# GLU as seven block products, forms mixed where the outputs are made, and banks kept for the last stage

## The chip, the core and the metric

The kernel runs on one core of one Trainium2 chip. Its engines work side by side and meet through semaphores: TensorE (PE) multiplies, VectorE (DVE) and ScalarE (ACT) work on tiles, GpSimd (POOL) and SyncE (SP) mostly issue transfers, as ScalarE does too. The metric is the device time of one execution in microseconds (us), the median of some runs. The profile is of one execution of its own.

## The reference

One layer over 1024 prompt tokens and 8 sample tokens (1032 columns), all in float32. Two branches, retention with 8 heads and an S5 state space model, are each multiplied by a gate and projected, then merged. Cut to what matters here:

```python
def layer(x, pos, ...):
    h = rmsnorm(x, g_pre)
    proj = h @ w_in
    q, k, v, za, ub, zb, ga, gb = jnp.split(proj, splits, axis=-1)
    ya, s_ret_new = retention(q, k, v, pos, s_ret)
    ya = (ya * jax.nn.silu(za.astype(F32))).astype(x.dtype) @ w_pa
    yb, s_re_new, s_im_new = s5(ub, ...)       # y = gelu(y); y * sigmoid(y @ w_glu + b_glu)
    yb = (yb * jax.nn.silu(zb.astype(F32))).astype(x.dtype) @ w_pb
    merged = jax.nn.sigmoid(ga) * ya + jax.nn.sigmoid(gb) * yb
    out = merged @ w_out
    return x + rmsnorm(out, g_post), ...
```

`w_in` is 2048 x 10240, `w_glu` 1024 x 1024, `w_pa` and `w_pb` 1024 x 2048, `w_out` 2048 x 2048.

## The kernel before

Activations lie transposed, features on the partitions and the 1032 tokens along the row. A float32 matmul is made of three: weights and activations are each split into a high part (ScalarE copies to fp32r, `whi`) and a low part (VectorE subtracts, `wlo`), and high x high, high x low and low x high are added up in a PSUM bank. `linear` (L256 ff. for `split`, L209 to L211 for `three`) does this for plain products, in thirds of 384, 384 and 264 tokens.

Most of the work uses block products instead. `product` (L880 ff., its matmul is L892) takes pairs of output tiles, splits the tokens into two halves of 516 (`HT`), and makes a 2 x 2 block product with seven multiplications instead of eight (a scheme of Strassen's kind). For this the activations are kept as seven *forms* (`FORMS`: u1, t2, v1, t3, t1, t4, v2, sums and differences of the blocks u1, u2, v1, v2), in 16 tiles `a0` to `a15` (`qslot`); the weights are combined on VectorE (`prep`: s1 to s4), two products ahead. A step is one pair of output tiles, seven products of 24 matmuls of 258 columns. The results go through `evac_st` or `evac_p`, which add and subtract PSUM banks into the four output blocks 11, 22, 21, 12.

In order of time:

- the first `ub` tiles by `linear`; then `steps` (L813): 35 pairs of `w_in` columns, twice, once for each half (`kh` 0 and 1) of the 2048 inputs. The partial sums of `kh` 0 go to `pt_d` in DRAM, those of `kh` 1 are added to them by an accumulating transfer (L946), and four products later (`LAG`) the activation, the RoPE or the like is put to work through `at` and `late_work`.
- beside that, in `slot()` after each product, a background generator goes on: `s5_params` and `s5_all` (S5 itself), `order_y` (L1209, brings S5's output into token order and writes `yn_d`), and `retention` (L1159, heads 0 to 7; `head` is L1032). The first head loads its vT and kT itself, each later one was loaded by the head before it (`load_vk`, on POOL's queue).
- GLU (L1475 to L1478): eight output tiles by `linear` from eight split tiles of `yn_d` (`load_gy`, `split_gy`). Beside it `glu_forms` reads `ya_d` back and makes four of the seven forms for `w_pa` in place; the others go to `fa_d`, to be fetched.
- pa and pb: eight steps each. `make_forms` reads `yb_d` and writes `fb_d` in the pa steps; the forms are fetched by `stage` (POOL's queue) into a pool of eight buffers and split by `unstage` into their `a` tiles as the old forms are used up. `gated` multiplies by the gates and, in pb, adds pa's result; for the last pair (p = 7) three of four such additions run on GpSimd.
- the last stage: `out_rows` for tokens 640 and up (`linear`, one bank of 392 columns per output tile), `out_tokens` for token tiles 0 to 2 and 3 to 4 with weights as the moving operand. PSUM is laid out anew before it (L1622): three double banks `pst` and two `pms` before, then five `pmm` and three `pms`.

Buffers come from pools stacked from the left and the right of SBUF. A tile in a new pool waits until what lay there has been released. Weights for block products come through a pool `wst` of seven buffers, four per step, loaded by SP (`fetch`, L842).

Of the kernel before, what the change touches and what calls it, by code (L numbers as in the profile page):

```python
# [23 lines left out]
H = 8  # L24
# [54 lines left out]
def emit(ctx, tc, I, O):  # L79
# [63 lines left out]
    fb_d = dram("fb_d", [2, 4, 128, TOK])  # L143
    yb_d = dram("yb_d", [8, 128, TOK])
# [659 lines left out]
    wstack, wst = popen("wst", "right", 7)  # L804
# [21 lines left out]
    def stage(pool, kh, n, i, eng=P):  # L826
        r = stq[kh, n, i] = pool.tile([128, HT], F32, name="stg")
        if kh in (0, 1):
            src = fm_d[kh, n, i]
        else:  # L830
            y, F = (ya_d, fa_d) if kh == "pa" else (yb_d, fb_d)
# [178 lines left out]
    def ret_const():  # L1010
        for n, shape in (("col", [128, 4, H]), ("mask", [128, 128])):
# [8 lines left out]
        K["a"] = act.tile([128, 2, TOK], F32, name="a12")  # L1020
        K["b"] = act.tile([128, 2, TOK], F32, name="a13")
# [3 lines left out]
    def load_vk(h):  # L1025
        vT, kT = R("vT", [128, TOK]), R("kT", [128, TOK], 2)
        P.dma_start(vT, v_d[h])
        for a in range(2):
            P.dma_start(kT[64 * a:64 * a + 64], kq_d[0, h // 2, a, 64 * (h % 2):64 * (h % 2) + 64])
        return vT, kT  # L1030

    def head(h):  # L1032
# [4 lines left out]
        vT, kT = K.pop("next") if h else load_vk(h)  # L1037
# [89 lines left out]
        if h + 1 < H:  # L1127
            K["next"] = load_vk(h + 1)
# [16 lines left out]
        oo = R("ktS", [128, TOK])  # L1145
# [12 lines left out]

    def retention():  # L1159
        ret_const()  # L1160
        for h in range(H):
            yield from head(h)
# [36 lines left out]
    TAGS = [12, 13, 14, 15] + list(range(12))  # L1199
    xs = {}  # L1200

    def xs_new(k):
        xs[k] = act.tile([128, 2, TOK], F32R, name=f"a{TAGS[k]}")
        return xs[k]

    gys = []
    gyr = {}

    def order_y():  # L1209
        for m in range(8):  # L1210
# [6 lines left out]
            o = k2p["pool"].tile([128, TOK], F32, name="yo", bufs=1)  # L1217
# [7 lines left out]

    def load_gy(m):
        gyr[m] = gp.tile([128, TOK], F32, name="gy")
        nc.sync.dma_start(gyr[m], yn_d[m])

    def split_gy(m):  # L1230
        t = xs_new(m)
        split((t[:, 0, :], t[:, 1, :]), gyr.pop(m))
        gys.append(t)
# [9 lines left out]
    e = 2 * NP - 1  # L1243
    when = {(e - 1, 4): (0,), (e - 1, 5): (1,), (e, 0): (2,), (e, 1): (3, 4), (e, 2): (5,), (e, 3): (6,), (e, 4): (7,)}
    for s in range(2 * NP):
# [35 lines left out]
        if s == 2 * NP - 2:  # L1281
            drain()
            rstack.close()
            gstack, gp = popen("gp", "left", 6)
            for m in range(6):
                load_gy(m)
        for n in range(7):
# [4 lines left out]
            if s == e and n == 5:  # L1292
                todo.extend((I["w_glu"], m, kq) for m in range(8) for kq in range(2))
                fetch_w()
# [15 lines left out]
            if (s, n) in when:  # L1310
                for m in when[s, n]:
                    at(g, lambda m=m: split_gy(m))
                    if m < 2:
                        at(g, lambda m=m: load_gy(6 + m))
            late_work(g)
            slot()
    gstack.close()

    def left_over():
        for n in range(12):  # L1320
            yield
            for g in sorted(due):
                if n >= {1: 4, 2: 6, 3: 9}[g - 14 * NP]:
                    late_work(g)


    bglu = const.tile([128, 8], F32, name="bglu")
    A.dma_start(bglu, I["b_glu"])
    gpost = const.tile([128, KD], F32, name="gpost")
    A.dma_start(gpost, I["g_post"])  # L1330
    zstack, zzp = popen("zz", "left", 4)
    zz_tile = lambda: zzp.tile([128, HT], F32, name="zz")
    opened = {}

    def fx_open():
        opened["fx"], opened["fxp"] = popen("fx", "left", 4)

    def stg_open(bufs):
        opened["stg"], opened["stgp"] = popen("stg3", "left", bufs)

    def glu_forms():
        t = {}

        def ld(i):
            t[i] = [opened["fxp"].tile([128, TOK], F32, name="fx") for _ in range(2)]
            for x, k in zip(t[i], (i, 4 + i)):
                P.dma_start(x, ya_d[k])

        ld(0)
        ld(1)  # L1350
        for _ in range(10):
            yield
        for i in range(4):
            u, v = t.pop(i)
            u1, u2, v1, v2 = u[:, 0:HT], u[:, HT:TOK], v[:, 0:HT], v[:, HT:TOK]
            split(qslot("pa", 0, i), u1)
            sub(u1, u1, u2)
            yield
            split(qslot("pa", 2, i), v1)
            sub(u2, u2, v2)  # L1360
            yield
            add(v2, v2, u1)
            P.dma_start(fa_d[0, i, :, 0:HT], u1)
            split(qslot("pa", 1, i), v2)
            yield
            sub(v1, v1, v2)
            P.dma_start(fa_d[1, i, :, 0:HT], v1)
            split(qslot("pa", 3, i), u2)
            yield
            if i < 2:  # L1370
                yield
                yield
                ld(i + 2)
            yield
        opened["fx"].close()
        stg_open(8)
        for o in order_q[16:24]:
            stage(opened["stgp"], "pa", *o)

    def make_forms(src, F):  # L1380
# [12 lines left out]
        for i in range(4):  # L1393
            u, v = t.pop(i)
            u1, u2, v1, v2 = u[:, 0:HT], u[:, HT:TOK], v[:, 0:HT], v[:, HT:TOK]
            sub(u1, u1, u2)
            sub(u2, u2, v2)
            yield
            add(v2, v2, u1)
            sub(v1, v1, v2)  # L1400
            P.dma_start(F[0, i], u)
            P.dma_start(F[1, i], v)
# [7 lines left out]

    zyq = deque()

    def load_zy(k):
        if k < 24:
            t0, t1 = THIRDS[k % 3]
            z = zz_tile()[:, 0:t1 - t0]
            zyq.append(z)
            P.dma_start(z, zy_d[k // 3, :, t0:t1])

    def evac_glu(m):  # L1420
        def f(t, ps):
            t0, t1 = THIRDS[t]
            s = ETILE(("p1", "u2", "u3")[t])[:, 0:t1 - t0]
            A.activation(s, ps, AF.Sigmoid, bias=bglu[:, m:m + 1])
            mul(s, s, zyq.popleft())
            P.dma_start(yb_d[m, :, t0:t1], s)
            load_zy(3 * m + t + 4)
        return f

    def both():  # L1430
        a, b = left_over(), glu_forms()
        n = 0
        while True:
            live = False
            for x in (a, b):
                try:
                    next(x)
                    live = True
                except StopIteration:
                    pass  # L1440
# [443 lines left out]
```

## Time and profile before

| | |
|---|---|
| median of three runs | 2610.0 us |
| the runs | 2617.08, 2610.0, 2609.98 us |
| the profiled execution | 2613.67 us |
| its span | 2611.9 us |
| VectorE, ScalarE, GpSimd busy | 71%, 37%, 26% of the span |
| DMA moved | 500.25 MB, mean 192 GB/s |

A span runs from the first to the last recorded instruction; the execution's time has a little around it. In rows of groups a line number is that of the helper that emits the operation (L84 is every `tensor_tensor`), so the names of the tiles tell what it is: `wlo<-wraw,whi` is the low part of a weight, `u<-acc,p` an evacuation. Matmuls overlap in the records, each lasting longer than the distance to the next; a rate is counts over the length of a stretch. The stages of the second half lie, in us from the start of the span, about so: `kh` 1 from 1020, retention 1350 to 1772, GLU 1819 to 1909, pa and pb to 2232, `out_rows` to 2373, `out_tokens` to 2600.

### The profile page before, as it was taken

How to read it: one execution, taken by the hardware profiler on the slowest of the kernel's cores; microseconds unless marked ns; L12 is line 12 of the kernel's file. 1: busy time of each engine (PE TensorE's matmuls, PEld its weight loads, DVE VectorE, ACT ScalarE, POOL GpSimd, SP SyncE). 2: the span in 40 equal slices, each digit the busy share in tenths (PEclk: the TensorE clock that was granted, in tenths of full speed). 3: DMA queues.
4: the chain of work that ended last, by engine and by line, in shares of the span. 5: the costliest groups of instructions: out<-in, count | busy, mean ns of one | idle time of the engine just before them, and what ended most of it. 6: DMA issues, size and time to landing. Idle time of an engine off the chain costs nothing.

```text
span 2611.9 us, 51326 instructions
## 1 busy us (share of the span) xinstructions
PE 2588.0 (99%) x19652; PEld 2531.1 (97%) x19652; DVE 1856.4 (71%) x3872; ACT 956.0 (37%) x1679; POOL 688.8 (26%) x1137
## 2 busy tenths in 40 slices
PE   9999999999999999999999999999999999999998
PEld 8999999999999999999999999999999999998886
DVE  7655988898898877558877666666577878544555
ACT  6113232333323324443234444445332422443344
POOL 0103322222222222332234434333422221111011
PEclk9999999999999999999999999999999999999999
DMA  6896534444444447886778878778867786655666
GB/s 192 257 265 217 154 111 125 138 120 124 129 122 131 131 127 245 207 206 168 164 192 241 231 197 209 206 196 250 273 226 255 232 230 212 215 166 182 187 200 227
DMA packets 229909, 500.25 MB, mean 192 GB/s; under 512 B 32432, under 2 KB 54912, under 8 KB 229536
## 3 DMA queue, kind: packets, MB, share of 16 engines
q0 software_dynamic: 90352, 263.82, 36.2%
q1 hardware_dynamic: 103072, 179.57, 22.5%
q10 hardware_dynamic: 36240, 53.60, 7.0%
q8 instruction: 154, 2.52, 0.4%
q14 instruction: 91, 0.75, 0.1%
HBM read 340.57 MB, written 156.30 MB: 190 GB/s over the span
## 4 chain that ended last, share of the span: by engine, by line
PE 97%; DVE 1%; issue 1%; DMA 1%; ACT 0%; DVEq 0%; SPq 0%; POOLq 0%; POOL 0%; ACTq 0%
PE acc L892 65%; PE mm L1782 7%; PE mm L209 5%; PE mm L210 5%; PE mm L211 5%; PE misc L1782 2%; PE acc L209 1%; PE acc L210 1%; PE acc L211 1%; PE misc L634 1%; PE misc L712 1%; PE misc L711 1%; PE misc L1099 1%; PE misc L1089 1%; PE misc L1068 1%
## 5 line engine op out<-in xcount | busy, mean ns | idle before, releaser
L892 PE MATMUL acc<-a,whi 128*128 128x258 f32 x9632 | 1561.4, 284 | 1.0 <-ACT whi L873 0.6
L892 PEld LDWEIGHTS acc<-a,whi 128*128 128x128 f32 x9632 | 1325.8, 190 | 5.2 <-issue 2.6
L892 PE MATMUL acc<-a,wlo 128*128 128x258 f32 x4816 | 969.1, 282 | 0.0
L892 PEld LDWEIGHTS acc<-a,wlo 128*128 128x128 f32 x4816 | 744.7, 189 | 0.0
L84 DVE TENSOR_TENSOR wlo<-wraw,whi 128x512 fp32r<-128x512 f32 x482 | 332.0, 689 | 237.9 <-ACT whi L202 138.1
L873 ACT CAST whi<-wraw 128x512 fp32r<-128x512 f32 x344 | 213.5, 621 | 619.6 <-PE acc L892 481.1
L873 ACT CAST whi<-wr 128x512 fp32r<-128x512 f32 x258 | 160.0, 620 | 507.4 <-PE acc L892 445.3
L209 PE MATMUL mm<-a,whi 128*128 128x384 f32 (+2 forms) x704 | 234.2, 334 | 8.6 <-ACT whi L202 5.2
L210 PE MATMUL mm<-a,whi 128*128 128x384 f32 (+2 forms) x704 | 233.7, 332 | 0.0
L211 PE MATMUL mm<-a,wlo 128*128 128x384 f32 (+2 forms) x704 | 232.2, 330 | 0.0
L84 DVE TENSOR_TENSOR wlo<-wr,whi 128x512 fp32r<-128x512 f32 x273 | 187.2, 686 | 51.6 <-ACT whi L873 30.0
L1782 PE MATMUL mm<-whi,a 128*128 128x512 f32 x512 | 171.1, 395 | 0.0
L202 ACT CAST whi<-wraw 128x512 fp32r<-128x512 f32 x138 | 85.5, 620 | 208.2 <-PE mm L210 104.1
L209 PEld LDWEIGHTS mm<-a,whi 128*128 128x128 f32 x704 | 133.6, 190 | 9.2 <-ACT whi L202 5.2
L211 PEld LDWEIGHTS mm<-a,wlo 128*128 128x128 f32 x704 | 133.9, 190 | 0.4 <-DVE wlo L84 0.2
L210 PEld LDWEIGHTS mm<-a,whi 128*128 128x128 f32 x704 | 133.3, 189 | 0.4 <-DVE a L363 0.4
L84 DVE TENSOR_TENSOR wraw<-wr 128x512 f32<-128x512 f32 x172 | 118.1, 686 | 2.9 <-DMA wr<-in_w_pa 0.6
L1782 PEld LDWEIGHTS mm<-whi,a 128*128 128x128 f32 x512 | 96.1, 188 | 22.8
L84 DVE TENSOR_TENSOR p<-acc,p 128x516 f32<-128x516 f32 x86 | 59.6, 692 | 70.9 <-PE acc L892 70.7
L84 DVE TENSOR_TENSOR wlo<-wx,whi 128x512 fp32r<-128x512 f32 x76 | 52.5, 692 | 71.4 <-ACT whi L202 71.1
L84 DVE TENSOR_TENSOR u<-acc,u 128x516 f32<-128x516 f32 x86 | 59.7, 694 | 60.0 <-PE acc L892 58.7
L84 DVE TENSOR_TENSOR u<-acc,p 128x516 f32<-128x516 f32 x86 | 59.5, 692 | 59.0 <-PE acc L892 58.7
(374 smaller groups left out, 3449.3 us busy)
## 6 DMA issues: line engine op xcount, KB each, us to landing
wr<-in_w_in SPq DMA_DIRECT2D x280, 256.0 KB
pt_d<-u POOLq DMA_DIRECT2D x70, 258.0 KB, 3.2
u<-pt_d POOLq DMA_DIRECT2D x70, 258.0 KB, 5.3
wraw<-in_w_outB SPq DMA_DIRECT2D x66, 256.0 KB
stg<-fm_d POOLq DMA_DIRECT2D x44, 258.0 KB, 4.5
wx<-in_w_outB SPq DMA_DIRECT2D x43, 256.0 KB
wraw<-in_w_out SPq DMA_DIRECT2D x39, 256.0 KB
pt_d<-st POOLq DMA_DIRECT2D x35, 258.0 KB, 3.3
```

Of the source, the lines that this page charges most:

```text
L84: return (eng or V).tensor_tensor(out, a, b, op)
L202: anchor["a"] = A.copy(hi, raw).ins
L209: T.matmul(ps, wh[:, i, :], xh[:, t0:t1], start=first, stop=False)
L210: T.matmul(ps, wh[:, i, :], xl[:, t0:t1], start=False, stop=False)
L211: anchor["p"] = T.matmul(ps, wl[:, i, :], xh[:, t0:t1], start=False, stop=last).ins
L634: T.matmul(ps[0:16, g * 128:(g + 1) * 128], B1[:, g, :], W3[:, g, 0:8, :], start=True, stop=True)
L711: T.matmul(o, Tm[:, g, :], U[:, g, 0:136], start=True, stop=False)
L712: T.matmul(o, W3[:, g, 1:9, :], X[:, g, 0:136], start=False, stop=True)
L873: anchor["a"] = A.copy(hi, f).ins
L892: anchor["p"] = T.matmul(ps[:, j, 0:258], a[:, i, :], b[:, 258 * j:258 * j + 258], start=first and i == 0 and a is wh and b is xh, stop=n ...
L1068: T.matmul(ps[:, c * 128:(c + 1) * 128], kt[:, 4 * i + c, :], vt[:, 4 * i + c, :], start=True, stop=True)
L1782: anchor["p"] = T.matmul(ps[c], a, b, start=k == 0 and a is xh and b is wh, stop=k == KD - 1 and a is xl).ins
```

## The change

GLU becomes four steps of block products between `kh` 1 and pa, with forms from `yn_d` and `fg_d`. The forms are mixed where the outputs are still in SBUF: `order_y` and `retention` take tiles or heads in the order 0, 4, 1, 5, 2, 6, 3, 7, and after each second one `mix` makes the sums of the pair and writes them to `fg_d` or `fa_d`. `transition` replaces the special code for fetching forms: into GLU, into pa and into pb alike, two loads and two splits per product. `wst` has five buffers instead of seven. The last stage stays on the banks `pst` and `pms`; each group of `out_tokens` takes one double bank and, for three token tiles, half of another.

```diff
-    wstack, wst = popen("wst", "right", 7)
+    wstack, wst = popen("wst", "right", 5)
...
-    steps = [(kh, p) for kh in range(2) for p in range(NP)] + [(kh, p) for kh in ("pa", "pb") for p in range(8)]
-    lim = [14 * NP]
+    steps = [(kh, p) for kh in range(2) for p in range(NP)] + [(kh, p) for kh, n in (("glu", 4), ("pa", 8), ("pb", 8)) for p in range(n)]
+    lim = [7 * len(steps)]
...
-        j = (2 * n + i // 2 + {0: 0, 1: -2, "pa": 4, "pb": 2}[kh]) % 16
+        j = (2 * n + i // 2 + {0: 0, 1: -2, "glu": -4, "pa": -6, "pb": -8}[kh]) % 16
...
     def ret_const():
+        K["a"] = act.tile([128, 2, TOK], F32, name="a12")
+        K["b"] = act.tile([128, 2, TOK], F32, name="a13")
+        K["next"] = load_vk(0, A)
         for n, shape in (("col", [128, 4, H]), ("mask", [128, 128])):
...
-        vT, kT = K.pop("next") if h else load_vk(h)
+        vT, kT = K.pop("next")
...
-        if h + 1 < H:
-            K["next"] = load_vk(h + 1)
+        if h != HEADS[-1]:
+            K["next"] = load_vk(HEADS[HEADS.index(h) + 1])
...
-        oo = R("ktS", [128, TOK])
+        oo = K["oo", h] = rstd if h < 4 else R("oo", [128, TOK])
...
+    HEADS = [0, 4, 1, 5, 2, 6, 3, 7]
+
     def retention():
         ret_const()
-        for h in range(H):
-            yield from head(h)
+        f = iter(())
+        for h in HEADS:
+            for _ in head(h):
+                yield
+                next(f, None)
+            if h > 3:
+                f = mix(K["oo", h - 4], K["oo", h], fa_d, h - 4)
+        for _ in f:
+            yield
...
+    def mix_a(u, v):
+        sub(u[:, 0:HT], u[:, 0:HT], u[:, HT:TOK])
+        sub(u[:, HT:TOK], u[:, HT:TOK], v[:, HT:TOK])
+
+    def mix_b(u, v, F, i):
+        add(v[:, HT:TOK], v[:, HT:TOK], u[:, 0:HT])
+        sub(v[:, 0:HT], v[:, 0:HT], v[:, HT:TOK])
+        P.dma_start(F[0, i], u)
+        P.dma_start(F[1, i], v)
+
+    def mix(u, v, F, i):
+        for _ in range(3):
+            yield
+        mix_a(u, v)
+        yield
+        mix_b(u, v, F, i)
+        yield
...
-        for m in range(8):
+        for m in (0, 4, 1, 5, 2, 6, 3, 7):
...
+            if m > 3:
+                yield from mix(yo[m - 4], yo[m], fg_d, m - 4)
...
+    def transition(g, base, kind):
+
+        q = g - 7 * base
+        n = moved.setdefault(kind, [0, 0])
+
+        def load():
+            at(g, lambda o=order_q[n[0]]: stage(opened["stgp"], kind, *o))
+            n[0] += 1
+
+        if 0 <= q < 4:
+            load()
+            load()
+        if 3 <= q < 20:
+            for i in range(1 if q < 7 else 2):
+                if n[1] < 28:
+                    at(g, lambda o=order_q[n[1]]: unstage(kind, *o))
+                    n[1] += 1
+                    if n[0] < 28:
+                        load()
...
-    raw_of["pool"] = wst
-    for m in range(8):
-        linear(I["w_glu"], m, 8, pair(gys), evac_glu(m), tick=glu_tick(m))
-    drain()
-    raw_of.clear()
...
-        if kind == "pb" and p > 1:
+        if kind == "pb" and p > 1 and (p < 7 or c):
...
+        if kind == "glu":
+            def times():
+                mul(t, t, z)
+                P.dma_start(yb_d[m, :, cols], t)
+
+            A.activation(t if ps is None else two(t), t if ps is None else ps, AF.Sigmoid, bias=bglu[:, m:m + 1])
+            at(g + 1, times)
+            return
...
-            add(t, t, zq.pop((name, "p")), P if p == 7 and name != "12" else V)
+            add(t, t, zq.pop((name, "p")), V)
...
-        a = act.tile([128, 2, TOK], F32R, name=f"a{m}")
+        a = act.tile([128, 2, TOK], F32R, name=f"a{(6 + m) % 16}")
...
+            transition(g, 2 * NP - 2, "glu")
+            transition(g, SG + 2, "pa")
+            transition(g, SB - 2, "pb")
...
-    psum_layout(("pmm", 5), ("pms", 3))
...
-            ps = [mmbank() if c < 2 else misc() for c in range(nch)]
+            both_ = banks_of["pst"].tile([128, 2, 512], F32, name="acc")
+            ps = [both_[:, 0, :], both_[:, 1, :]]
+            if nch == 3:
+                ps.append(mmbank())
             steps = [[(k, c) for c in range(nch)] for k in range(KD)]
             if last and g == 3:
+                ps[1] = mmbank()
                 steps[13:] = [[(k, c) for k in (13, 14, 15)] for c in range(nch)]
+            elif not last:
+                steps[14:] = [[(k, c) for k in (14, 15)] for c in range(nch)]
```

Here `SG` is the first GLU step (70), `SA` = `SG` + 4 the first of pa and `SB` = `SG` + 12 the first of pb. Gone with GLU's `linear` are `load_gy`, `split_gy`, `glu_forms`, `load_zy`, `evac_glu` and their helpers.

More of the change, by code (lines that the diff above doesn't have):

```diff
@@ L143, in emit @@
     fb_d = dram("fb_d", [2, 4, 128, TOK])
+    fg_d = dram("fg_d", [2, 4, 128, TOK])
     yb_d = dram("yb_d", [8, 128, TOK])
@@ L1198, in emit @@
     k2p = {}
[L1199 to L1207, printed above, removed]
+    def mix_a(u, v):
[13 more added lines that the diff above has]
+        yield
     def order_y():
-        for m in range(8):
+        yo = {}
+        for m in (0, 4, 1, 5, 2, 6, 3, 7):
             r = k2p["pool"].tile([128, TOK], F32, name="yr", bufs=1)
@@ L1216, in order_y @@
                 yield
-            o = k2p["pool"].tile([128, TOK], F32, name="yo", bufs=1)
+            o = yo[m] = k2p["pool"].tile([128, TOK], F32, name="yo", bufs=2)
             for c in range(2):
@@ L1242, in emit, with fx_open, stg_open @@
     nxt = done_q = 0
-    e = 2 * NP - 1
-    when = {(e - 1, 4): (0,), (e - 1, 5): (1,), (e, 0): (2,), (e, 1): (3, 4), (e, 2): (5,), (e, 3): (6,), (e, 4): (7,)}
+    bglu = const.tile([128, 8], F32, name="bglu")
+    A.dma_start(bglu, I["b_glu"])
+    gpost = const.tile([128, KD], F32, name="gpost")
+    A.dma_start(gpost, I["g_post"])
+    opened, moved = {}, {}
+    def fx_open():
+        opened["fx"], opened["fxp"] = popen("fx", "left", 4)
+    def stg_open(bufs):
+        opened["stg"], opened["stgp"] = popen("stg3", "left", bufs)
+    def transition(g, base, kind):
[14 more added lines that the diff above has]
+                        load()
     for s in range(2 * NP):
@@ L1283, in emit @@
             rstack.close()
-            gstack, gp = popen("gp", "left", 6)
-            for m in range(6):
-                load_gy(m)
+            zstack, zzp = popen("zz", "left", 4)
+            stg_open(8)
         for n in range(7):
@@ L1409, in make_forms @@
         opened["fx"].close()
[L1411 to L1440, printed above, removed]
-            if not live:
-                return
-            yield
-    def tail_forms():
-        for k in (1, 1, 2):
-            for _ in range(k):
-                unstage("pa", *order_q[pa_q[0]])
-                if pa_q[0] + 8 < 28:
-                    stage(opened["stgp"], "pa", *order_q[pa_q[0] + 8])
-                pa_q[0] += 1
-            yield
-    pa_q = [16]
-    pair = lambda L: (lambda k: (L[k][:, 0, :], L[k][:, 1, :]))
-    for k in range(4):
-        load_zy(k)
-    fx_open()
-    bg.append(both())
-    S0 = 2 * NP
-    lim[0] = 7 * len(steps)
-    def glu_tick(m):
-        def f(kq, t):
-            if m == 7 and kq == 0 and t == 2:
-                drain()
-                bg.append(tail_forms())
-                fetch(S0)
-            if m == 7 and kq == 1 and t < 2:
-                prep(7 * S0 + t)
-            if t < 2 or kq == 1:
-                slot()
-        return f
-    raw_of["pool"] = wst
-    for m in range(8):
-        linear(I["w_glu"], m, 8, pair(gys), evac_glu(m), tick=glu_tick(m))
-    drain()
-    raw_of.clear()
     zq = {}
```

122 lines of the change are left out of this document (15 added, 107 removed).

## The prediction

> **What bounds the kernel now.** I read the page first: busy time by engine, then the shares of the chain of work that ended last, then the list of whatever the TensorE waited for in the whole program.
>
> ```profile
> span 2611.9 us, 51326 instructions
> PE 2588.0 (99%) x19652; PEld 2531.1 (97%) x19652; DVE 1856.4 (71%) x3872; ACT 956.0 (37%) x1679; POOL 688.8 (26%) x1137
> PE 97%; DVE 1%; issue 1%; DMA 1%; ACT 0%; DVEq 0%; SPq 0%; POOLq 0%; POOL 0%; ACTq 0%
> ```
> ```profile
> PE mm L209 <- ACT whi L202: 5.2, 1, 5.2
> PE mm L209 <- DVE u L84: 2.8, 1, 2.8
> PE misc L1049 <- ACT a L1047: 2.2, 1, 2.2
> PE acc L892 <- ACT whi L873: 0.6, 1, 0.6
> PE mm L209 <- ACT a L362: 0.5, 1, 0.5
> PE acc L892 <- DVE u L84: 0.3, 2, 0.2
> ```
>
> The reader is to see that TensorE (PE) is busy for 2588 of 2611.9 us, and that its waits add up to 11.6 us, of which the first and the fifth row, 5.7 us, are the start-up (the first weights and the first x). So there are only two ways to gain: fewer matmul columns, or one of the two waits of 2.8 and 2.2 us. And there is one way to lose: a new wait of PE. What the other engines do is free as long as PE doesn't notice.
>
> The windows view of the stretches that matter (start:end; length, then busy time and count for PE, PE weight load, VectorE, ScalarE, GpSimd; granted clock, DMA share, GB/s):
>
> ```profile
> 1818.77:1909.38 90.61, 90.61 (x580) 90.61 (x579) 47.17 (x79) 34.70 (x63) 39.88 (x74) 1.00 0.76 252
> 1909.38:2232.04 322.66, 322.66 (x2689) 322.45 (x2687) 254.96 (x400) 103.36 (x179) 68.59 (x118) 1.00 0.76 239
> 2234.87:2238.64 3.77, 3.77 (x12) 3.77 (x13) 2.74 (x5) 0.00 (x0) 0.54 (x1) 0.55 0.66 221
> 1240.00:1260.00 20.00, 20.00 (x169) 20.00 (x168) 17.28 (x29) 5.32 (x9) 5.73 (x8) 1.00 0.68 156
> 1760.00:1780.00 20.00, 20.00 (x167) 19.81 (x166) 13.39 (x34) 10.41 (x22) 8.38 (x11) 1.00 0.61 157
> 1800.00:1818.00 18.00, 18.00 (x152) 18.00 (x152) 14.03 (x18) 12.54 (x18) 7.20 (x13) 1.00 0.81 214
> 2000.00:2020.00 20.00, 20.00 (x169) 20.00 (x168) 12.88 (x21) 4.84 (x8) 1.99 (x5) 1.00 0.50 157
> 2060.00:2080.00 20.00, 20.00 (x169) 20.00 (x168) 19.96 (x34) 12.02 (x23) 7.91 (x15) 1.00 0.96 318
> ```
>
> **GLU as block products.** The first row is today's GLU: 90.61 us with no gap. Its matmuls by shape, for one of its three lines, then those of the stage after it:
>
> ```profile
> L209 PE MATMUL acc<-a,whi 128*128 128x384 f32 x128 | 43.1, 336 | 0.0
> L209 PE MATMUL acc<-a,whi 128*128 128x264 f32 x64 | 18.3, 286 | 0.0
> L892 PE MATMUL acc<-a,whi 128*128 128x258 f32 x1792 | 288.2, 283 | 0.0
> L892 PE MATMUL acc<-a,wlo 128*128 128x258 f32 x896 | 179.9, 282 | 0.0
> ```
>
> That is 3 x 192 = 576 matmuls, 198,144 columns. The change makes 4 pairs of output tiles x 7 products x 4 blocks x 3 parts x 2 halves = 672 matmuls of 258 columns, 173,376 columns, seven eighths. The pa and pb stage is made of just these: 1792 + 896 = 2688 in 322.66 us, or 0.1200 us each (the mean durations in the rows overlap and are no rate). 672 x 0.1200 = 80.7 us; the saving is **9.9 us**. It is on PE, so on the path; nothing hides it.
>
> What VectorE and ScalarE do for it must stay beside PE. One step of 7 products (7 x 24 x 0.1200 = 20.2 us) asks VectorE for 7 splits, 4 weight sums, 7 evacuations and 4 gate products, 22 operations. Such operations follow each other at 0.61 us (the starts of the two rows at 1437.46 and 1438.06 below), so 13.4 us. In the transition that fetches the forms there are 2 splits per product more, 14 x 0.61 = 8.5, together 21.9 us in 20.2. That is over the mark, but the last window row is this very load, the pb transition: VectorE 19.96 of 20.00 busy, PE 20.00. ScalarE had 12.02; GLU's four sigmoids of a step fit into the other 8. So I cost the two new transitions (into GLU, into pa) at nothing on both. If the cover of two products' lookahead is gone, the excess, 1.7 us each, is what it costs.
>
> Their transfers are another matter. At two loads of 258 KB per product the pb transition raises the DMA share from 0.50 to 0.96, by 0.46. The transition into GLU falls into the last gb steps, whose own share lies between 0.61 and 0.81 (the rows at 1760, which has retention in it, and at 1800, which has other loads in it): 1.07 to 1.27 for the 8 products at two loads, 23 us, which leaves 1.6 to 6.2 us of transfers late. The late one that hurts is the accumulating read of the partial sum:
>
> ```profile
> u<-pt_d POOLq DMA_DIRECT2D x5, 258.0 KB, 7.7
> ```
>
> That median of 7.7 us is from 1776 to 1912; ScalarE asks for it four products, 11.5 us, after issue, and has a product's time (2.9 us) before PE notices. Bounds 0 to 6.2 us; I take 1, nearer to the pb row, which had no wait.
>
> **Banks kept.** The 2.8 us wait is the handover from pst to pmm/pms:
>
> ```profile
> 2231.64 0.40 PE L892 MATMUL acc<-a,wlo 128*128 128x258 f32 x2
> 2234.87 0.48 PE L209 MATMUL mm<-a,whi 128*128 128x392 f32 x1 [2.83 <-DVE u L84]
> 2238.64 0.34 PE L209 MATMUL mm<-a,whi 128*128 128x392 f32 x1
> 2239.17 0.34 PE L209 MATMUL mm<-a,whi 128*128 128x392 f32 x1
> ```
> ```profile
> 2232.36 1.76 DVE L84 TENSOR_TENSOR wlo<-wraw,whi 128x512 fp32r<-128x512 f32 x1
> 2234.04 0.68 DVE L84 TENSOR_TENSOR u<-acc,u 128x516 f32<-128x516 f32 x1
> 2232.05 1.52 POOL L84 TENSOR_TENSOR p<-p,pp 128x516 f32<-128x516 f32 x1 [1.35 <-DVE p L84]
> ```
>
> The first matmul of w_out needs a bank that the last evacuation (u<-acc) frees, and that stood in VectorE's queue behind a split which took 1.76 us instead of 0.68 (the row at 1438.06 below) while GpSimd was adding. Behind the gap the granted clock is 0.55: 12 matmuls took 3.77 us, at the later pace ((2239.17 - 2238.64)/3 = 0.177) they take 2.12. The handover costs 2.83 + 1.65 = 4.5 us. With the banks kept, w_out's first bank is one that was freed four products earlier, and GpSimd's three adds are gone (two become accumulating DMAs, one goes to VectorE). What is late next is the low part of the first w_out weights, the split itself: begun at 2232.36 and not stretched it is done at 2233.0, and PE wants it two matmuls after 2232.04 (2231.64 + 0.40), at 2232.4. The queue ahead of it is shorter, too; I leave 0.4 us: **-4.1 us**; bounds 0 (the wait only changes its name) and -4.5.
>
> The Trainium skill, page "TensorE: Matmul & The Clock Gate", section "Why this matters for your kernels", asks only that there be no idle gaps over about 3 us, since a window of idle lowers the clock. By that rule a gap of 2.83 us would not have cost the clock, and this part would bring 2.4. The trace differs: the clock is halved right behind this gap; the measurement decides.
>
> In the last stage three double banks take turns. At the end of each weight group the last two blocks are taken token tile by token tile, 6 matmuls each, so the second half of a double bank is done 6 matmuls, 1.4 us, before the group ends and wanted 1.4 us after the next begins. Its evacuation is one ScalarE and one VectorE operation of 0.6 to 0.7 us. That fits: 0.
>
> **Retention.** The 2.2 us wait stands at the first head:
>
> ```profile
> 1347.88 0.58 POOL L1013 DMA_DIRECT2D col<-in_col  x1 [1.33 <-DMA kq_d<-pl]
> 1349.51 0.53 POOL L1027 DMA_DIRECT2D vT<-v_d  x1
> 1352.65 0.87 POOL L946 DMA_DIRECT2D st<-pt_d  x1 [1.00 <-ACT st L988]
> 1362.65 1.28 ACT L966 ACT_TABLE_LOAD   x1 [2.16 <-DMA st<-pt_d]
> ```
>
> ScalarE waited for the partial sum, which took 10 us from its issue at 1352.65 behind constants, vT and kT on POOL's queue; the copy that frees PE's misc bank stood behind it. The change issues vT and kT (three transfers, 1 MB) ahead of the constants and from ScalarE's queue. That unloads POOL's queue, but all wait for kq_d<-pl as col did (1347.88), and a ScalarE that stands there holds up the next split and evacuation. Bounds -2.2 and +1.5; I take **-1.0**.
>
> The Trainium skill, page "DMA: Bandwidth & Descriptors", section "Issuing engines are not separate DMA queues", says that transfers from any issuing engine share the same 16 DMA engines, so only issue time is saved. By it this term is 0 and the sum 1.0 us smaller; no row here shows the two cases side by side.
>
> The mixing is 16 subtractions and additions of 516 for S5 and 16 for retention, in pairs of 1.2 us. For S5 they fall into stretches where VectorE has at least 2.7 us idle in 20 (the row at 1240): 0. For retention three of four fall ahead of the scores, VectorE's tightest place in a head:
>
> ```profile
> 1437.46 0.68 DVE L84 TENSOR_TENSOR u<-u,acc 128x516 f32<-128x516 f32 x1
> 1438.06 0.68 DVE L84 TENSOR_TENSOR wlo<-wr,whi 128x512 fp32r<-128x512 f32 x1
> 1443.28 0.70 DVE L84 TENSOR_TENSOR p<-acc,p 128x516 f32<-128x516 f32 x1 [3.40 <-PE acc L892]
> ```
>
> There 2.4 us more stand against an idle 3.40 us that comes only afterwards: 0 to 1.5 each; I take 0.3 x 3, **+1**. The fourth is issued in one piece when the retention ends; PE has matmuls enough: 0. The order of heads adds no work.
>
> **The sum.** -9.9 - 4.1 - 1.0 + 1 + 1 = **-13.0 us**. Against the profiled execution (2613.67 us, span 2611.9, so 1.8 us around it) that is 2600.7, span 2598.9. The profiled execution lies 3.7 us above the median of 2610.0, whose other runs were 2609.98 and 2617.08; against the median it is **2597.0 us**.
>
> **Rivals.** (1) *The bank wait changes its name.* The w_out weights' low part, or ScalarE standing at the load of the merged tiles until the last mg_d store has landed, halts PE instead. For it: the gap was made by VectorE's queue, and that keeps its order. Against: three adds are gone from GpSimd. Without the 4.1: 2601. (2) *The transfers into GLU are late.* Shares over 1 for 23 us; PE waits the full 6.2 us and the clock halves once behind a gap (1.7): 2597 - 1 + 7.9 = 2604. (3) *Slower: five weight buffers instead of seven.* Then the fourth weight tile of a step is fetched only when the split for its sixth product has read the buffer, one product into the second half, and is wanted 4 products later: 11.5 us, less 1.3 for the split, leaves 10.2 until VectorE and ScalarE stand. It is the one edit that acts in all of 88 steps. It decides from 10.2 us landing time on: each 0.3 us that PE waits per step is 26 us, 2597 + 26 = 2623. Against it are the page's medians for transfers of that size, and in the most crowded stretch st<-pt_d took 10:
>
> ```profile
> pt_d<-u POOLq DMA_DIRECT2D x70, 258.0 KB, 3.2
> u<-pt_d POOLq DMA_DIRECT2D x70, 258.0 KB, 5.3
> ```
>
> (4) *GLU brings nothing*, were the stage bound elsewhere: its PE row has no idle, so I give it no chance of its own.
>
> **How the numbers follow.** Forecast 0.62; rival 1 0.18; rival 2 0.14; rival 3 0.04; 0.02 for something unseen. The forecast's own ends: -9.9 - 4.5 - 2.2 = 2593.4 below; above, half of the unknown costs, 2601. The range reaches to rivals 1 and 2: 2592 to 2605. A measurement can tell about 0.3%, 7.8 us, from no change: faster means under 2602.2, which is the forecast, most of rival 1: 0.81; same is rival 2 and the rest of 1: 0.14; slower 0.05.
>
> **What would show it.** GLU about 80.7 us of L892 between the last gb product and the first pa product; no gap and a clock of 1.00 at the start of w_out; a list of PE's waits without the 2.8. Wrong would be: PE waiting for whi or wlo with a wr transfer behind it in many steps (rival 3), for an accumulating read in the two steps ahead of GLU (rival 2), or a gap before the first w_out matmuls (rival 1).

## The result and the profile after

The changed kernel takes 2624.1 us (median of 5 runs, 2621.2 to 2625.6) against 2610.3 of the kernel before on the same chip: a ratio of 1.0045, 95% interval 1.0034 to 1.0057. It is slower, by 12 us by the ratio and 14 by the medians; the forecast was 13 us faster, and the time lies outside its range, 2592 to 2605. The profiled execution took 2625.6 us, 1.5 above the median; that of the kernel before lies 3.4 above its own, so that a difference of two traces can be a few us off that of the medians. The page of after:

```profile
span 2623.8 us, 51705 instructions
PE 2587.1 (99%) x19748; PEld 2523.9 (96%) x19748; DVE 1895.2 (72%) x3949; ACT 968.9 (37%) x1707; POOL 693.3 (26%) x1145
...
L84 DVE TENSOR_TENSOR wraw<-wr 128x512 f32<-128x512 f32 x180 | 123.3, 685 | 28.6 <-DMA wr<-in_w_in 22.9
```

TensorE is busy for only 0.9 us less than before, although 25 thousand columns are gone; 11.0 us of its busy time are now at half clock, 3.4 before. The last row is new: VectorE stands 22.9 us for weights that haven't landed, at the sums of two weight tiles. TensorE's own list of waits (us in total, times, longest):

```profile
PE acc L893 <- DVE u L84: 10.6, 8, 2.7
PE acc L893 <- DVE wlo L84: 5.5, 2, 4.9
PE acc L893 <- ACT p L983: 1.8, 1, 1.8
PE acc L212 <- DVE wlo L84: 0.7, 1, 0.7
```

The 2.8 and 2.2 us of before are gone; 18.6 us of others have come. Where they lie is read by counting matmuls: a step of block products has 168, so the time at which each step starts can be compared in the two traces.

| stretch | before, us | after, us | difference |
|---|---|---|---|
| start to step 45 | 1221.6 | 1221.8 | +0.1 |
| steps 45 to 50 (rotation of q and k) | 121.0 | 132.9 | **+11.9** |
| step 51 (retention's first head) | 24.4 | 31.4 | **+7.0** |
| steps 52 to 67 | 411.5 | 412.0 | +0.5 |
| step 68 (end of retention) | 20.2 | 24.3 | **+4.1** |
| step 69 and GLU | 110.6 | 100.8 | **-9.8** |
| pa and pb | 322.8 | 324.0 | +1.1 |
| handover and `out_rows` | 142.2 | 138.6 | **-3.6** |
| `out_tokens` | 225.6 | 227.4 | +1.8 |
| after the last matmul | 12.0 | 10.7 | -1.4 |

GLU and the two parts of the last stage as windows of after, and the last stage of before (columns as in the prediction):

```profile
1842.50:1923.12 80.62, 80.62 (x674) 80.62 (x673) 66.99 (x106) 45.69 (x78) 26.05 (x49) 1.00 0.81 267
2247.14:2385.78 138.64, 137.90 (x770) 137.58 (x769) 60.62 (x88) 63.46 (x112) 16.95 (x18) 1.00 0.57 177
2385.78:2613.18 227.40, 227.34 (x977) 181.10 (x976) 125.53 (x217) 90.59 (x166) 30.66 (x54) 1.00 0.66 206
```
```profile
2232.04:2374.28 142.24, 139.41 (x769) 139.44 (x769) 61.79 (x88) 63.77 (x112) 18.28 (x18) 0.99 0.53 170
2374.28:2599.87 225.59, 225.58 (x977) 182.01 (x976) 125.44 (x217) 91.37 (x166) 30.62 (x54) 1.00 0.67 207
```

So the two gains came, 13.4 us, and three new losses, 23.1 us, ate them. Each is a place where an engine stands with its queue behind it. In the rotation stretch of after:

```profile
1226.04 0.69 DVE L84 TENSOR_TENSOR wraw<-wr,wraw 128x512 f32<-128x512 f32 x1
1231.14 0.69 DVE L84 TENSOR_TENSOR wraw<-wr 128x512 f32<-128x512 f32 x1 [4.40 <-DMA wr<-in_w_in]
1231.75 0.68 DVE L84 TENSOR_TENSOR u<-p,acc 128x516 f32<-128x516 f32 x1
1232.48 0.75 PE L893 MATMUL acc<-a,whi 128*128 128x258 f32 x4 [1.90 <-DVE u L84]
```

The sum at 1231.14 is `s1` of the *next* step, five products ahead of the first that needs it (through `s2`). It waits for a weight tile, and the evacuation `u<-p,acc` behind it frees TensorE's bank late. At retention's first head:

```profile
1361.42 0.33 ACTq L1029 DMA_DIRECT2D vT<-v_d  x1
1361.85 0.59 ACT L983 COPY p<-acc 128x516 f32<-128x516 f32 x1 [6.55 <-DVE mhalf L1019]
1362.90 0.55 POOL L1021 DMA_DIRECT2D selr<-in_sel  x1
1370.15 0.20 DVE L1023 CAST sel<-selr 128x64 fp32r<-128x64 f32 x1 [6.99 <-DMA selr<-in_sel]
1370.26 0.68 DVE L84 TENSOR_TENSOR wlo<-wraw,whi 128x512 fp32r<-128x512 f32 x1
```
```profile
1348.98 0.54 POOL L1017 DMA_DIRECT2D selr<-in_sel  x1
1352.67 0.20 DVE L1019 CAST sel<-selr 128x64 fp32r<-128x64 f32 x1 [1.06 <-DMA selr<-in_sel]
```

The second fence is the kernel before. After the change the last constant is issued behind the 1 MB of v and k and is there 7.25 us after its issue, not 3.7; VectorE stands at its cast with a weight split behind it. At the end of retention, in after:

```profile
1802.58 0.70 DVE L84 TENSOR_TENSOR oo<-oo,rstd 128x516 f32<-128x516 f32 x1 [4.55 <-DMA ya_d<-oo]
...
1804.78 0.84 POOL L1218 DMA_DIRECT2D fa_d<-oo  x1
1810.67 2.14 POOL L836 DMA_DIRECT2D stg<-yn_d  x4 [4.51 <-issue]
...
1814.41 0.62 ACT L257 CAST a<-stg 128x516 fp32r<-128x516 f32 x1 [5.15 <-issue]
...
1815.06 0.70 DVE L84 TENSOR_TENSOR a<-stg,a 128x516 fp32r<-128x516 f32 x1 [5.39 <-ACT a L257]
...
1815.67 0.69 DVE L84 TENSOR_TENSOR u<-acc,p 128x516 f32<-128x516 f32 x1
```

(`issue` means that the profile shows nothing that was waited for.) The last mix overwrites `oo` while it is still being stored, and the stage loads behind it come late: VectorE stands 5.4 us at the first split into the GLU products, with an evacuation behind it, and TensorE 2.7 us. The store `fa_d<-oo` landed at 1810.06, 0.6 us before the first stage load was issued; in two kernels with an earlier last mix (2623.7 and 2602.8 below) it is 0.6 us again.

### The profile page after: what moved, and what is told of

It is laid out like the page before. It is cut to its first block, busy times and chain, and to the rows that moved or that the text cites. A ratio compares the mean times of both kernels' runs of the same rounds, so it can differ in the third digit from the quotient of the medians.

```text
span 2623.8 us, 51705 instructions
## 1 busy us (share of the span) xinstructions
PE 2587.1 (99%) x19748; PEld 2523.9 (96%) x19748; DVE 1895.2 (72%) x3949; ACT 968.9 (37%) x1707; POOL 693.3 (26%) x1145
## 5 line engine op out<-in xcount | busy, mean ns | idle before, releaser
L893 PE MATMUL acc<-a,whi 128*128 128x258 f32 x10080 | 1638.7, 284 | 13.3 <-DVE u L84 10.6
L893 PEld LDWEIGHTS acc<-a,whi 128*128 128x128 f32 x10080 | 1390.9, 190 | 19.9 <-DVE u L84 8.8
L893 PE MATMUL acc<-a,wlo 128*128 128x258 f32 x5040 | 1016.3, 283 | 5.5 <-DVE wlo L84 5.5
L84 DVE TENSOR_TENSOR wlo<-wraw,whi 128x512 fp32r<-128x512 f32 x496 | 339.8, 686 | 228.0 <-ACT whi L203 132.9
L1680 PE MATMUL acc<-whi,a 128*128 128x512 f32 x640 | 201.9, 396 | 0.0
L210 PE MATMUL mm<-a,whi 128*128 128x384 f32 (+1 forms) x448 | 145.0, 326 | 5.6 <-ACT whi L203 5.6
L1680 PEld LDWEIGHTS acc<-whi,a 128*128 128x128 f32 x640 | 120.2, 188 | 30.1 <-DVE z L84 1.9
L211 PE MATMUL mm<-a,whi 128*128 128x384 f32 (+1 forms) x448 | 145.2, 324 | 0.2 <-DVE a L364 0.2
L212 PE MATMUL mm<-a,wlo 128*128 128x384 f32 (+1 forms) x448 | 144.9, 323 | 0.3 <-DVE wlo L84 0.2
L84 DVE TENSOR_TENSOR wraw<-wr 128x512 f32<-128x512 f32 x180 | 123.3, 685 | 28.6 <-DMA wr<-in_w_in 22.9
L1680 PE MATMUL acc<-wlo,a 128*128 128x512 f32 x320 | 127.0, 397 | 0.0
L84 DVE TENSOR_TENSOR a<-stg,a 128x516 fp32r<-128x516 f32 x140 | 91.7, 688 | 12.8 <-ACT a L257 12.7
L203 ACT CAST whi<-wx 128x512 fp32r<-128x512 f32 x78 | 48.4, 620 | 128.4 <-PE acc L1680 45.0
```

Of the source, the lines that this page charges most:

```text
L84: return (eng or V).tensor_tensor(out, a, b, op)
L203: anchor["a"] = A.copy(hi, raw).ins
L210: T.matmul(ps, wh[:, i, :], xh[:, t0:t1], start=first, stop=False)
L211: T.matmul(ps, wh[:, i, :], xl[:, t0:t1], start=False, stop=False)
L212: anchor["p"] = T.matmul(ps, wl[:, i, :], xh[:, t0:t1], start=False, stop=last).ins
L893: anchor["p"] = T.matmul(ps[:, j, 0:258], a[:, i, :], b[:, 258 * j:258 * j + 258], start=first and i == 0 and a is wh and b is xh, stop=n ...
```

## The experiments

### The rotation stretch

**Five buffers in the kernel before**, and nothing else:

```diff
-    wstack, wst = popen("wst", "right", 7)
+    wstack, wst = popen("wst", "right", 5)
```

> The kernel before with five weight buffers in place of seven, nothing else. Theory (buffers): the sums s1 and s2 of the next step stand five products ahead of where they are needed in VectorE's order, so their tiles 21 and 22 must have landed a whole step early; with five buffers they are asked for one tile's life later and VectorE stands at them, with the evacuation behind it. Then this kernel loses about as much as the changed one did in the six steps from 1212 to 1355: 10 to 12 us, so 2620 to 2622, with TensorE gaps of about 2 us that end with an evacuation u<-p,acc, and VectorE waiting for wr. Rival (mixing): the six waits come from the additional S5 mixing on VectorE in that stretch; then this kernel, which has no mixing there, stays within 3 us of 2610 and shows no gap there.

2617.4 us, ratio 1.0029 (1.0016 to 1.0042): +6.7, steps 45 to 50 +7.5. VectorE's waits there are those of after; the kernel before has none:

```profile
DVE wraw L84 <- DMA wr<-in_w_in: 19.1, 7, 4.4
```

The buffers are a cause by themselves, at two thirds of the expected size in this run.

**Two more buffers in that stretch**, on the changed kernel:

```diff
+            wpool = wsx["p"] if wsx and s <= NP + 15 and wn[0] % 7 > 4 else wst
-            raws[s, n] = wst.tile([128, 4, 128], F32, name="wr")
+            raws[s, n] = wpool.tile([128, 4, 128], F32, name="wr")
...
+            wsx["st"], wsx["p"] = popen("wsx", "left", 2)
...
```

> The changed kernel with two further weight buffers only while the sine and cosine rotation of q and k runs (steps 36 to 50), in memory that is free there; the S5 mixing stays. Theory (buffers): the gaps of TensorE between 1212 and 1355 go, the stretch from step 45 to 51 is 10 to 12 us shorter, and the time is 2612 to 2614. Rival (mixing): the gaps stay, within 3 us of 2624. What follows, the start of retention and the end of it, keeps its own gaps by both.

2610.8 us, ratio 1.0000 (0.9991 to 1.0010): 13 us gained, and steps 45 to 50 are as long as before (0.0), as they are in the four later kernels that have these buffers. The whole 11.9 us hang on the buffers.

**The S5 mixes.** Two kernels ask why the loss is larger in the changed kernel than in the one before with five buffers. One leaves out the S5 mixes' sums, one their stores too:

```diff
-                yield from mix(yo[m - 4], yo[m], fg_d, m - 4)
+                for _ in range(4):
+                    yield
+                P.dma_start(fg_d[0, m - 4], yo[m - 4])
+                P.dma_start(fg_d[1, m - 4], yo[m])
+                yield
```

> The changed kernel with five weight buffers, in which the S5 outputs are stored unmixed: the 16 additions and subtractions of the S5 mixes on VectorE are left out, their stores stay. The kernel before with five buffers lost 7.1 us between steps 45 and 51, the changed kernel 12.0. Theory (VectorE): the other 5 us are the mixes standing ahead of the evacuations on a VectorE that is already late; without them the stretch loses 7, and the time is 2618 to 2620. Rival (transfers): the stores of the mixed forms, 4 MB that the kernel before does not have there, make the weights land later; then the stretch still loses 11 to 12 us.

> The changed kernel with five weight buffers and neither the 16 sums of the S5 mixes nor their 4 MB of stores; the GLU products read the unmixed S5 outputs in place of the mixed ones. It tells whether the larger loss in the changed kernel (13 us by the two more buffers) than in the kernel before with five buffers (7 us) comes from these transfers. Theory (transfers): 2617 to 2619, as the stretch loses about 7. Rival (not the mixes at all): within 2 us of 2624; the sums alone left out gave 2622.7.

2622.7 (1.0042; 1.0027 to 1.0058) and 2620.7 (1.0034; 1.0022 to 1.0047), steps 45 to 50 +8.5 and +4.7. But six kernels whose code is the same up to step 50, the changed one among them, lost 6.4 to 14.3 us there. The intervals overlap that of the changed kernel: how much the mixes add is not settled.

**The weight sums held** behind the last split, with five buffers:

```diff
+            with tc.issue_after(anchor["v"]):
-            add(r[s, name], r[s, a], r[s, b])
+                add(r[s, name], r[s, a], r[s, b])
```

> The changed kernel, still with five weight buffers, with the weight sums s1, s2, s3 and s4 held on VectorE behind the last split that was issued ahead of them; s1 of the next step then stands ahead of the evacuation of product 5 and no longer of product 1. Theory (early sums): it is not that weights land too late for their products, but that VectorE's order asks for them four to five products early; held, the gaps between 1212 and 1355 go, that stretch is 9 to 12 us shorter, and the time is 2612 to 2615, as with two more buffers. Rival (late weights): five buffers are too few in themselves there; the gaps stay or move to another evacuation, and the time is within 3 us of 2624.

2625.7 (1.0058; 1.0046 to 1.0071): no gain, as the rival had it. But its trace has no wait for a weight between 1200 and 1350, and steps 45 to 50 lost 4.3. What was gained there went elsewhere: 4.8 us were lost by step 45, where two evacuations came 1.4 and 1.3 us late in the S5 stretch, and a gap of 3.0 us with the halved clock behind it came at the handover. The first head kept its loss, 7.6 us. So the sums were held only in the rotation stretch, in a kernel that also has the two mends tried below:

```diff
+            with ExitStack() as held:
+                if NP + 2 <= s <= NP + 15:
+                    held.enter_context(tc.issue_after(anchor["v"]))
...
```

> Five weight buffers, the weight sums held only in the rotation stretch (steps 37 to 50), the first head's v and k loaded after the constants from GpSimd's queue, the last mix begun at once. Theory (early sums): the sums' place in VectorE's order is the whole cause of the loss there, so this equals the kernel with two more buffers and the same two mends, 2601 to 2605, with steps 45 to 51 within 2 us of the kernel before. Rival (two causes): with five buffers ScalarE's splits come late too (a 2.3 us gap behind whi was left when all sums were held), the stretch keeps 4 us or more, 2606 to 2610.

2606.4 (0.9979; 0.9970 to 0.9988); steps 45 to 50 +4.4. VectorE's waits in 1200 to 1350, complete:

```profile
DVE wlo L84 <- ACT whi L877: 16.1, 26, 1.1
DVE u L84 <- PE acc L896: 2.3, 3, 1.7
```

In this stretch no weight is late for its product with five buffers; it is late for a sum that stands too early. The 4.4 are in the main one gap of 2.3 us and the halved clock behind it: the held sum `s2` came behind four sums of an S5 mix, and the split waited for it. Both theories had a part.

### The first head of retention

**The early load alone**, in the kernel before:

```diff
     def ret_const():
+        K["a"] = act.tile([128, 2, TOK], F32, name="a12")
+        K["b"] = act.tile([128, 2, TOK], F32, name="a13")
+        K["next"] = load_vk(0, A)
...
```

> The kernel before with only the first head's v and k moved ahead of the constants and to ScalarE's queue, as the change does it. Theory (order): TensorE's gap of 2.2 us at the first head becomes one or two of together 5 to 7 us, part of it behind a split that waits for the cast of the last constant, and the clock is halved behind it: 5 to 8 us slower, 2615 to 2618. Rival (crowding by the rest of the change): within 2 us of 2610, the 2.2 us wait gone or the same. The prediction had put this part at -1.0, from -2.2 to +1.5.

2618.6 (1.0031; 1.0020 to 1.0042): +8 (+5 between the profiled executions), step 51 +5.1. The same picture as in after:

```profile
1347.80 0.59 ACT L982 COPY p<-acc 128x516 f32<-128x516 f32 x1 [4.76 <-DVE mhalf L1018]
1356.15 0.20 DVE L1022 CAST sel<-selr 128x64 fp32r<-128x64 f32 x1 [6.96 <-DMA selr<-in_sel]
1356.99 0.58 PE L892 MATMUL acc<-a,wlo 128*128 128x258 f32 x1 [4.93 <-DVE wlo L84]
```

**Three ways to undo it** in the changed kernel: loading behind the constants from GpSimd's queue; behind them, but from ScalarE's; ahead of them, but from GpSimd's (`load_vk(0, P)`).

```diff
-        K["next"] = load_vk(0, A)
...
         V.tensor_copy(K["sel"], selr.rearrange("p (b c) -> p b c", b=8))
...
+        K["next"] = load_vk(0, P)
```

> The changed kernel with the first head's v and k loaded as before: after the constants, from GpSimd's queue. Theory (order): the early 1 MB of v and k, put ahead of the constants, makes the last constant land late, and VectorE stands at its cast with a weight split behind it; undone, the step from 1355 to 1386 is 6 to 8 us shorter, one wait of about 2 us at the first head is left, and the time is 2616 to 2618. Rival (crowding): the constants are late because the weights and partial sums of this kernel crowd the transfers there, whatever the order; then less than 2 us is gained.

> The changed kernel with the constants issued first, and the first head's v and k still from ScalarE's queue: it tells the order from the queue. Theory (order): what costs is the 1 MB ahead of the last constant, so this gives as much as loading them from GpSimd behind the constants did, 2616 to 2619, and no wait behind the cast of the last constant. Rival (queue): ScalarE standing at an issue that waits for the rotated k costs the time, so it stays within 2 us of 2624.

> The changed kernel with the first head's v and k still ahead of the constants, but from GpSimd's queue. Theory (order): 1 MB ahead of the last constant is enough; VectorE's cast is late by 4 us or more, TensorE stops behind the split, and the time stays at 2622 to 2625; ScalarE's copy no longer waits, which is worth at most 2 us. Rival (queue): ScalarE's queue is what costs, and with GpSimd's queue the step from 1355 to 1386 is 6 us shorter, 2616 to 2618.

2618.3 (1.0024; 1.0013 to 1.0036), 2621.7 (1.0044; 1.0028 to 1.0059) and 2617.0 (1.0022; 1.0013 to 1.0031); step 51: -2.1, +7.8, -0.4. My theory of the order fell twice. Behind the constants in the program is not behind them on the chip when the queue is another one: ScalarE issued v at 1354.4, GpSimd the first constant at 1354.8. And ahead of them it costs nothing in step 51 from GpSimd's queue, although the last constant is just as late:

```profile
1355.77 0.58 ACT L983 COPY p<-acc 128x516 f32<-128x516 f32 x1
1362.11 0.56 POOL L1021 DMA_DIRECT2D selr<-in_sel  x1
1365.14 0.69 DVE L84 TENSOR_TENSOR u<-acc,p 128x516 f32<-128x516 f32 x1 [1.31 <-PE acc L893]
1369.74 0.19 DVE L1023 CAST sel<-selr 128x64 fp32r<-128x64 f32 x1 [3.90 <-DMA selr<-in_sel]
```

It landed after 7.6 us, but in this kernel's order of VectorE the cast stands behind the evacuation of product 3, not of product 1, and ScalarE's copy doesn't wait. That the load makes the constant late holds throughout: in the ten kernels that issue v ahead of it, it landed 6.7 to 8.4 us after its issue, in the nine others 2.9 to 4.6.

**The cast moved** five products later, the load as the change has it:

```diff
             for _ in range(5):
                 yield
+            V.tensor_copy(sel, K["selr"].rearrange("p (b c) -> p b c", b=8))
...
```

> The changed kernel with v and k still loaded ahead of the constants from ScalarE's queue, and only the cast of the last constant on VectorE moved five products later, to where the first head begins. Theory (the cast blocks): TensorE's 4.9 us behind the split that stands behind that cast go, and the halved clock behind them; the step from 1355 to 1386 is 4 to 6 us shorter and the time is 2618 to 2620. The 1.8 us wait for ScalarE's copy, which stands at the loads, stays. Rival (the engines are late anyhow, since weights or partial sums crowd): the gap moves to the next operation and the time stays within 2 us of 2624.

2617.6 (1.0024; 1.0015 to 1.0033): 6.5 us gained, step 51 0.0; of TensorE's waits there, 1.3 us behind ScalarE's copy and 0.6 at the first transpose are left. A late constant is not what cost, but the place of its cast ahead of a split.

### The end of retention

```diff
-        for _ in range(3):
+        for _ in range(0 if F is fa_d and i == 3 else 3):
             yield
         mix_a(u, v)
```

> The changed kernel with the last mix of the retention begun at once, not three products later, so that it is no longer issued in one piece when the retention is closed. Theory (piece): the second half of that mix overwrites oo while oo is still being stored, VectorE stands 4.6 us there with an evacuation behind it, and the memory comes free late; issued sooner, the 4.2 us that step 68 lost go to under 1.5, and the time is 2620 to 2621. Rival (crowding): the transfers into the GLU products are what is late there; then less than 1 us is gained.

2623.7 (1.0046; 1.0030 to 1.0061): step 68 went from +4.1 to +1.6, but GLU gave most of it back. The rival's number holds; its cause, crowded transfers, is not shown. A later start of the splits into GLU, on the mended kernel below:

```diff
-        if 3 <= q < 20:
+        if (5 if kind == "glu" else 3) <= q < 20:
```

> The kernel with the three mends (2602.8) and the first two splits into the GLU products two products later. Theory (loads behind the store): the stage loads wait until the last mix has been stored, land four products on, and the split that waits for them holds up an evacuation; later splits cost nothing and leave no gap around step 68 and 69. In that kernel the gap was already closed, so at most 0.5 us is gained: 2602 to 2603. Rival: the late splits crowd VectorE ahead of the first GLU product and a gap of 1 to 3 us appears at step 70: 2604 to 2606.

2605.2 (0.9977; 0.9967 to 0.9987): 2.4 us above that kernel, which the two intervals don't separate, with gaps of 0.7, 0.7 and 1.4 us from 1807 on; nothing gained, nearer to the rival. What a mended end is worth alone stays open. Step 68 lost 0.0 to 3.8 us in the seven kernels with the mix begun at once, 1.4 to 5.3 in the nine other versions of the changed kernel, but step 69 and GLU gained less in most of the seven (5.4 to 9.8, against 9.8 in each of the nine).

### The banks, and versions that gain

**Three mends together**: two more buffers in the rotation stretch, loading behind the constants from GpSimd, the last mix at once.

> The changed kernel with the two further weight buffers in the rotation stretch, the constants ahead of the first head's v and k on GpSimd's queue, and the last mix begun at once. If the three losses are separate, it takes about 13, 6 and 3 us off 2624: 2601 to 2604, faster than both kernels, which leaves the gain of the block products and of the kept banks. If they share one cause (transfers that crowd everywhere), mending one moves the wait to the next and it stays at 2608 to 2612.

2602.8 us, ratio 0.9968 (0.9956 to 0.9979): faster than both kernels. The losses add up much as separate ones do: alone the three mends gave 13.3, 5.8 and 0.4 us, together 21.3. **The same with the sums held** everywhere in place of the buffers, and **the three mends with the old banks**:

```diff
+    psum_layout(("pmm", 5), ("pms", 3))
...
+            ps = [mmbank() if c < 2 else misc() for c in range(nch)]
```

> The changed kernel with the sums held, the constants ahead of the first head's v and k on GpSimd's queue, and the last mix begun at once; five weight buffers. If holding the sums is worth as much as two more buffers, it takes 2601 to 2604 like the kernel that has these; it can be better by 1 us, since the wait for a weight in the second step of the pa products (1.3 us there) goes too. If late weights are the limit in themselves, it stays at 2610 or above.

> The kernel with the three mends and the banks laid out anew for the last stage, as before the change. By the traces the handover gap of 2.8 us and the halved clock behind it (1.7 us) come back in place of 1.0 us, and the 1.8 us that the last rows lost by waiting for a half of a double bank go: +1.7 us, 2604 to 2605. If the longer last rows have another cause, +3.5 us, 2606.

Sums held everywhere: 2619.8 (1.0034; 1.0021 to 1.0046), with the losses of holding as above, 5.9 us by step 45 and a gap of 2.5 us at the handover. Old banks: 2603.4 (0.9971; 0.9959 to 0.9982), no difference that the intervals can tell. The handover is back in it, but the clock was not halved behind it:

```profile
2227.92 0.42 PE L210 MATMUL mm<-a,whi 128*128 128x392 f32 x1 [2.80 <-DVE u L84]
```
```profile
2227.92:2237.92 10.00, 10.00 (x56) 10.00 (x57) 5.33 (x9) 3.57 (x7) 1.64 (x3) 1.00 0.77 244
2365.82:2591.40 225.58, 225.58 (x977) 181.97 (x976) 125.42 (x217) 91.34 (x166) 30.58 (x54) 1.00 0.66 207
```

And `out_tokens` takes 225.6 us as before the change. With the banks kept, TensorE's weight loads wait there for evacuations (`z`) and for splits (`wlo`), here in after; with the old banks, here and in the kernel before, no such wait is over 0.2 us:

```profile
PEld acc L1680 <- DVE z L84: 1.9, 6, 0.3
PEld acc L1680 <- DVE wlo L84: 1.9, 5, 0.5
```

**One sum held in five steps**, on the mended kernel, which still waited for weights at the first head and in the second pa step:

```diff
+                if name == "s1" and s in (NP + 16, NP + 17, NP + 18, 2 * NP + 5, 2 * NP + 6):
+                    held.enter_context(tc.issue_after(anchor["v"]))
```

> The kernel with the three mends (2602.8) in which the sum s1 alone is held on VectorE in five steps: the three around the first head (51 to 53) and the two of pa where a wait for weights was left (75 and 76). Theory (early sums): the gaps of 1.8 us with its halved clock at 1351 and of 1.3 us at 1930 go, 3 to 5 us: 2598 to 2600. Rival (late weights): the weights are late there in themselves, since the transfers of the first head and of the pa forms crowd them; the gaps stay or move to the product that needs the sum, 2602 to 2604.

2600.0 us, ratio 0.9958 (0.9945 to 0.9972), the fastest. TensorE's waits, the first rows:

```profile
PE mm L210 <- ACT whi L203: 5.6, 1, 5.6
PE acc L899 <- DVE u L84: 2.1, 5, 1.1
PE acc L899 <- ACT whi L880: 0.6, 1, 0.6
```

Beside the start 2.9 us are left, and neither wait is among them: the early sum was the cause at both places. The time is 2.8 us below that with the three mends, within what the two intervals allow for.

## Why the prediction was wrong, point by point

The two gains came, 13.4 of 14.0 us. What failed in the main are three terms, put at nothing or as a gain: the five buffers, retention's first head and the fourth mix. They cost 23.1 us, the five buffers more than half of it.

- **GLU, -9.9**: right. 672 matmuls in 80.62 us, 0.1200 each; -9.8 with step 69. No excess of VectorE showed inside it.
- **Banks, -4.1**: the handover gave -3.6; the gap left was 0.7 us, not 0.4. The step that failed is "That fits: 0" for the last stage: +1.8. Weight loads wait 3.8 us there for evacuations and splits; which of these makes it is not shown. And the 1.65 us of halved clock in the term belonged to one execution: with the old banks a gap of 2.8 us came without it, and between those two traces the banks gained 1.8 us at the handover and lost 1.9 in `out_tokens`.
- **Retention's first head, -1.0, bounds -2.2 and +1.5**: +7.0 there, 8 us alone in the kernel before. I saw ScalarE stand, but didn't ask what VectorE has queued behind the constants that the 1 MB overtakes: a cast, a split behind it, and TensorE's 4.9 us. Moving the cast took 6.5 us back.
- **Five buffers** stood only in rival 3, at 0.04, on the fourth tile's 10.2 us of slack. The step that failed is the assumption that a weight sum runs where it is wanted. VectorE's order puts `s1` of the next step five products ahead, and its tiles have no such slack. The price fell not on 88 steps but on the six of the rotation, where it was 11.9 us. That the rival's 2623 us lies near the measured time is luck: its parts were others.
- **The fourth mix, "PE has matmuls enough: 0"**: step 68 lost 4.1. What was missed is the overwriting of a tile in store and the stage loads that wait for that store; mending it alone brought nothing measurable, so the size is not shown.
- **Transfers into GLU, +1**: the wait that was costed, for the accumulating read, didn't come, and no gap stands in the crowded stretch from 1820 to 1860. The late transfers were the stage loads themselves, and their 2.7 us are in what step 68 lost.
- **Retention's other mixes, +1**: the step starts moved by 0.5 us from 53 to 68, half of the term. **S5's mixes, 0**: not settled, 0 to 3 us.

With these three waits mended the kernel takes 2602.8 us, and with one sum held in five steps 2600.0, 3 us above the forecast.

## What to carry to other kernels

Where an order is fixed ahead of time, fewer buffers must be costed from the *first* instruction that reads the tile in the engine's order, read off the trace, not from the product that needs the result. A load that is moved ahead must be followed to what it overtakes, and from there to what stands behind the first reader of the overtaken; another engine's queue keeps no order with the one it left. A halved clock seen once behind a gap shorter than 3 us is a chance, not a price: it hangs on where the gap falls.

## What the runs showed of the hardware

The granted clock was halved for 3.4 us behind some gaps of TensorE and not behind others of the same length. In all these traces 33 gaps of 1.77 to 2.98 us stood by themselves: 20 were followed by it and 13, up to 2.82 us, were not. Of those of 0.9 to 1.7 us that stood alone none was, and all nine of 3.49 us and more were. Where the gap falls decides. Within a trace the clock changes only at whole multiples of 3.413 us from one another: in after it was halved from 1255.70, from 1300.07, which is 13 such lengths later, and from 1368.34, 20 more. Laid on that grid, each of the 20 gaps that were followed has at least 1.77 us inside one length, and each of the 13 others at most 1.80. Two of the handover show it: a gap of 2.82 us with 1.94 of it in one length was followed (the early load in the kernel before), one of 2.83 with at most 1.52 in one was not (five buffers in the kernel before). By these numbers a gap of 2.8 us would be followed in an estimated three quarters of its positions on the grid; of the four of that length seen at the handover two were. One in after, gap and what follows:

```profile
1297.59:1300.07 2.48, 0.01 (x2) 0.00 (x1) 1.35 (x3) 0.91 (x2) 0.85 (x1) 1.00 0.16 60
1300.07:1303.48 3.41, 3.41 (x16) 3.41 (x17) 3.41 (x6) 0.00 (x0) 0.00 (x0) 0.50 0.56 77
```

The Trainium skill, page "TensorE: Matmul & The Clock Gate", section "What's actually happening", has a free-running window of 3413 ns; the length agrees with the 3.41 us here, and that it runs by itself agrees with the grid. The limit of about 3 us for a gap, which the Trainium skill gives on the same page, section "Why this matters for your kernels", does not agree: 1.77 us was enough.
